# Two-layer hybrid trunk on one core: the second layer's gate projections first, their results kept in DRAM, and the triangular inverses moved wholly to VectorE beside them

## The chip, the cores and the metric

One core of a Trainium2 chip runs the whole program in one launch. The metric is the device time of that core in microseconds, as the median of three runs. TensorE (PE in the rows, PEld for its weight loads) multiplies matrices, VectorE (DVE) and ScalarE (ACT) do the elementwise work, GpSimd (POOL) does elementwise work and issues some DMAs, and SyncE's queue (SP) issues nearly all DMAs.

## What is computed

The trunk has two layers on a residual stream of 256 tokens by 2048 features, in float32. The second layer, which the change concerns, is:

```python
h = rms_norm(x, norm_g)
proj = einsum('btd,de->bte', h, w_in)                  # 2048 -> 18064 columns
q_c, ckv, z_c, iq, ik, iw, qkv, z_d, b_pre, a_pre = split_cols(proj, SPLIT_CD)
y_c = dsa_branch(q_c, ckv, z_c, ...)                   # sparse attention, 16 heads; ends  o * silu(z_c)
y_d = gdn_branch(qkv, z_d, b_pre, a_pre, ...)          # gated delta rule, 32 heads; ends  rms_norm(o) * silu(z_d)
x = x + einsum('bte,ed->btd', concatenate([y_c, y_d]), w_out)
```

The gates `silu(z_c)` (2048 columns) and `silu(z_d)` (4096 columns) are used only at the very end of each branch. The delta branch works in chunks of 64 tokens; in each chunk and head it solves a unit lower triangular 64 by 64 system:

```python
a_mat = where(strict, bc * kk * decay, 0.0)
sol = triangular_solve(eye + a_mat, concatenate([vb, kb]), lower=True, unit_diagonal=True)
```

With 32 heads and 4 chunks there are 128 such systems, one in each SBUF partition. The kernel forms the inverses and stores them.

## The kernel before

The kernel is one function that traces instructions for a planner: the planner gives each engine its own order, by the order in which instructions were traced and by its own estimate of when an operand is ready, and adds the waits. Matmuls that are traced inside `tick()` are pinned behind all matmuls traced before them; all others may be taken earlier when something ahead of them isn't ready.

Every projection multiplies float32 data as three fp32r products. `load_w` (line 179) loads 1 MB of weights into `wr` (3 buffers) on SP's queue, ScalarE casts them to `wh` and VectorE forms the rest `wl = wr - wh` (2 buffers each); both are traced at high priority. `proj_tok` (line 195) makes a 256-token by 512-column product with tokens in the partitions: for 2048 features 4 loads and 96 matmuls of 512 columns. `proj_feat` (line 227) makes its transpose: 4 loads and 192 matmuls of 256 columns. `out_proj` (line 343) takes 8 blocks of a finished unit through 4 times 512 columns of the output matrix, 192 matmuls of 512 columns in 8 loads, and adds to the residual.

Two kinds of background work are dealt into the projections. `steps` holds generators of which `tick()` (line 164) advances the first by one step; a projection calls `tick()` after each 4 (`proj_tok`: 2) blocks of matmuls, 16 times in a projection of 2048 features and 8 times for each 512 columns of `out_proj`. `flush()` runs all that is left. `lag(n)` is n empty steps. `bg` holds generators that `pump()` (line 151) advances by one step at each `load_w`; only the inverses are there.

The second layer's order is: keys, indexer, top-k and the latent `ckv`; then the inverses start (line 932); four attention groups; four delta groups of two halves; the last two output units and the final norm.

The inverses (lines 932 to 977) are 62 elimination steps on `U` (64 by 64 in each partition). Step s changes rows 0 to s-1 and columns s+1 to 63. POOL does the first 9 rows (`SPLIT = 9`), three instructions a step at lines 951, 952 and 954, all traced at once; VectorE does the other rows, two instructions a step at lines 962 and 964, one step at each `pump()` after four empty ones. At the end VectorE scales `U` (lines 968 and 970), POOL masks it (line 972), writes the diagonal (line 973) and stores it to `Wd` (line 974).

An attention group (line 990) projects queries `CQ` (192 matmuls), its keys and values from the latent (`w_uk`, `w_uv`, one load each), and its gate `CZC`; the generator `attend` (line 1017) runs four heads through logits, transposes and values, multiplies by the gate and turns the result into a unit. `qd`, `kd`, `vd` and `zc` have one buffer each, so a group waits for the group before to have ended its heads (line 992). Group 3 also does output unit 0.

A delta group i (line 1092) projects queries, and then for each half s: values (192 matmuls), `flush()`, the generator `delta` (line 1158), the gate `CZD` (96 matmuls, line 1246), and for s = 0 and i up to 2 the whole output unit i+1 (line 1251). `delta` is a chain: transposes `vt`, then for two 128-token parts the products `pu`, `pr`, `pu2`, `pog`, between them `pS`, `pks`, `pqs`, then a norm, the gate, and transposes `turn` (line 267).

Of the kernel before, what the change touches and what calls it, by code (L numbers as in the profile page):

```python
# [31 lines left out]
SPLIT = 9  # L32
# [3 lines left out]
LQ, LV, LS, LT = 7, 8, 2, 10  # L36
LH, LA = 3, 3
# [25 lines left out]
def trunk(ctx, tc, x, rel_bias, ab_norm, ab_w_in, ab_ml_b_i, ab_ml_b_f, ab_ml_norm, ab_ssm_conv_w,  # L63
# [107 lines left out]
    def lag(n):  # L171
        for _ in range(n):
            yield
# [550 lines left out]
    with ExitStack() as st:  # L724
# [189 lines left out]

        sv = ExitStack()
        sp = sv.enter_context(tc.tile_pool(name="sv", bufs=1))
        ap = sv.enter_context(tc.tile_pool(name="ap", bufs=1))

        cT = sp.tile([128, 4, 512], F32R, name="cT")
        cn = ap.tile([128, 2, 512], F32, name="cn", tag="zc")  # L920
        cs_ = ap.tile([128, 2], F32, name="cs_")
        cr = ap.tile([128, 2], F32, name="cr")
# [9 lines left out]
        U = sp.tile([128, 64, 64], F32, name="U")  # L932
        pl = sp.tile([128, 64], F32, name="pl")
# [8 lines left out]
        V.tensor_tensor(pl, pl, rl, op=OP.mult)  # L942
        V.tensor_tensor(wl_, pl, rl, op=OP.mult)  # L943
        V.tensor_scalar(nw, wl_, scalar1=-1.0, scalar2=None, op0=OP.mult)

        for s in range(1, 63):
            n, m = 63 - s, min(s, SPLIT)
            co = sp.tile([128, SPLIT], F32, name="co", tag="co")
            tmp = sp.tile([128, SPLIT * (63 - SPLIT)], F32, name="tmpg", tag="tmpg")
            tv = tmp[:, 0:m * n].rearrange("p (j l) -> p j l", j=m)  # L950
            G.tensor_scalar(co[:, 0:m], U[:, 0:m, s], scalar1=wl_[:, s:s + 1], scalar2=None, op0=OP.mult)  # L951
            G.tensor_tensor(tv, co[:, 0:m].unsqueeze(2).to_broadcast([128, m, n]),  # L952
                            U[:, s + 1:64, s].unsqueeze(1).to_broadcast([128, m, n]), op=OP.mult)
            G.tensor_tensor(U[:, 0:m, s + 1:64], U[:, 0:m, s + 1:64], tv, op=OP.subtract)  # L954

        def solve():
            yield from lag(LW)
            for s in range(SPLIT + 1, 63):
                n, m = 63 - s, s - SPLIT
                tmp = sp.tile([128, (63 - SPLIT) ** 2 // 4], F32, name="tmp", tag="tmp")  # L960
                tv = tmp[:, 0:m * n].rearrange("p (j l) -> p j l", j=m)
                V.scalar_tensor_tensor(tv, U[:, SPLIT:s, s:s + 1].to_broadcast([128, m, n]), wl_[:, s:s + 1],
                                       U[:, s + 1:64, s].unsqueeze(1).to_broadcast([128, m, n]), op0=OP.mult, op1=OP.mult)
                V.tensor_tensor(U[:, SPLIT:s, s + 1:64], U[:, SPLIT:s, s + 1:64], tv, op=OP.subtract)
                yield
            for i in range(4):
                Ui = U[:, i * 16:i * 16 + 16]
                V.tensor_tensor(Ui, Ui, nw.unsqueeze(1).to_broadcast([128, 16, 64]), op=OP.mult)
                yield
# [8 lines left out]

        Xc = [(cT, k) for k in range(4)]
# [6 lines left out]
        def out_unit(u, then=None):  # L986
            out_proj(cd_w_out, u * 1024, units[u], then)

        attended = []
        for g in range(4):  # L990
            pts = proj_feat(cd_w_in, 0, X, [(CQ + g * 512, 512, 0)])
            while len(attended) < g:
                tick()
            qd = ap.tile([128, 4, 256], F32, name="qd", tag="qd")
            for b in range(2):
                A.copy(qd[:, b * 2:b * 2 + 2].rearrange("p b t -> p (b t)"), pts[b])
            gated = []
            if g == 0:

                pts = proj_tok(cd_w_in, 0, X, CZC)  # L1000
                flush()
                zc = ap.tile([128, 2, 512], F32, name="zc", tag="zc")
                for t in range(2):
                    gate2(zc[:, t], pts[t])
                gated.append(True)
            pts = proj_feat(w_uk, 0, Xc, [(g * 512, 512, 0)])
            kd = ap.tile([128, 4, 256], F32, name="kd", tag="kd")
# [3 lines left out]
            vd = ap.tile([128, 2, 512], F32, name="vd", tag="vd")  # L1011
            A.copy(vd[:, 0], pts[0])
            A.copy(vd[:, 1], pts[1])
            if g:
                zc = ap.tile([128, 2, 512], F32, name="zc", tag="zc")

            def attend(g, qd, kd, vd, zc, gated):
# [51 lines left out]
                while not gated:  # L1069
                    yield  # L1070
# [7 lines left out]
            steps.append(attend(g, qd, kd, vd, zc, gated))  # L1078
            if g:
                pts = proj_tok(cd_w_in, 0, X, CZC + g * 512)  # L1080
                for t in range(2):
                    gate2(zc[:, t], pts[t])
                gated.append(True)
# [3 lines left out]
        if solving in bg:  # L1087
            drain(solving)
        sv.close()

        with tc.tile_pool(name="gp", bufs=1) as gp:
            for i in range(4):
# [23 lines left out]
                for s in range(2):  # L1116
# [39 lines left out]
                    gated = []  # L1156

                    def delta(s, h0, qc, kT, k0, QD, Wg, Kg, vf, o, z, rq, rq2, gated):
# [10 lines left out]
                        for t in range(2):  # L1169
                            A.activation(v[:, t], tp[t], AF.Copy, scale=0.5)  # L1170
                        yield from lag(LS)
# [62 lines left out]
                        while not gated:  # L1234
                            yield
# [87 lines left out]
```

## Time and profile before

| what | value |
|---|---|
| median of 3 runs | 2251.69 us (2250.92 to 2253.16) |
| the profiled execution | 2252.15 us |
| its span, first to last instruction | 2250.1 us |
| PE busy | 2148.8 us (95%) in 13006 matmuls |
| PEld busy | 1882.0 us (84%) |
| DVE busy | 1498.2 us (67%) |
| ACT busy | 999.1 us (44%) |
| POOL busy | 368.3 us (16%) |
| mean granted TensorE clock | 0.984 |
| HBM read, written | 382.51 MB, 19.03 MB |

The page gives busy times of each engine, the same in 40 equal slices of the span, the chain of waits that ended last, and groups of instructions. A matmul's busy time overlaps the next one's, so its price is the distance between two starts, not its mean. [...] The attention groups and the inverses lie between 1114 and 1425 us, the delta groups between 1425 and 2172 us.

### The profile page before, as it was taken

Reading aid. Unit: us, or ns where it says so; the run is one execution under the profiler, and the core shown is the slowest. Engines: PE = TensorE matmul, PEld = TensorE weight load, DVE = VectorE, ACT = ScalarE, POOL = GpSimd, SP = SyncE. Lnnn points to the kernel's source line nnn. Section 1 sums busy time; section 2 is a strip of 40 time slices with the busy share of each in tenths; the row PEclk is TensorE's granted clock in tenths of the full one; section 3 lists DMA queues with packets and bytes.
Section 4 is the critical chain, followed back from the end, with each engine's and each line's share of the span. In section 5 each row is a group of like instructions: output and inputs, shape, how many; then the busy total and the mean of one; then the engine's idle time right before and its main releaser. Section 6 shows DMA issues by size and latency. Waiting matters only on the chain.

```text
span 2250.1 us, 31828 instructions
## 1 busy us (share of the span) xinstructions
PE 2148.8 (95%) x13006; PEld 1882.0 (84%) x13006; DVE 1498.2 (67%) x2082; ACT 999.1 (44%) x1319; POOL 368.3 (16%) x352
## 2 busy tenths in 40 slices
PE   6999999999999998999967879999999999999997
PEld 6989997888788888988866768898997898888876
DVE  7898755545454557688699976565565657557655
ACT  5455444344434444556423335444454444345443
POOL 4000020000000003011399971000000000001001
PEclk9999999999999999999998989999999999999999
DMA  5655465555565554677833336665554554555443
GB/s 178 214 189 182 156 205 191 187 171 186 174 198 170 185 183 136 206 263 260 231 104 116 127 112 213 202 204 175 187 175 152 193 174 153 192 172 170 150 150 131
DMA packets 233992, 400.47 MB, mean 178 GB/s; under 512 B 39909, under 2 KB 63990, under 8 KB 232054
## 3 DMA queue, kind: packets, MB, share of 16 engines
q1 hardware_dynamic: 229046, 376.19, 51.0%
q0 software_dynamic: 4800, 22.25, 3.0%
q8 instruction: 102, 1.67, 0.3%
q14 instruction: 44, 0.36, 0.0%
HBM read 382.51 MB, written 19.03 MB: 178 GB/s over the span
## 4 chain that ended last, share of the span: by engine, by line
PE 77%; POOL 10%; DVE 4%; DMA 2%; ACT 2%; issue 1%; SPq 0%; ACTq 0%; DVEq 0%
PE pt L75 43%; PE pf L75 26%; POOL U L954 4%; POOL co L951 3%; POOL tmpg L952 3%; DVE wl L192 2%; PE pu L75 1%; ACT wh L191 1%; PE py L75 1%; DMA wr<-in_ab_w_in_dram 1%; DMA wr<-in_cd_w_in_dram 1%; PE turn L79 1%; PE pr L75 1%; PE pog L75 1%; PE si L75 1%
## 5 line engine op out<-in xcount | busy, mean ns | idle before, releaser
L192 DVE TENSOR_TENSOR wl<-wr,wh 128x2048 fp32r<-128x2048 f32 (+1 forms) x337 | 785.1, 2330 | 503.1 <-ACT wh L191 502.1
L191 ACT CAST wh<-wr 128x2048 fp32r<-128x2048 f32 (+1 forms) x337 | 639.3, 1897 | 769.7 <-PE pt L75 432.1
L75 PE MATMUL pf<-hT,wh 128*128 128x256 f32 x4192 | 771.5, 286 | 0.3 <-POOL hT L296 0.2
L75 PEld LDWEIGHTS pf<-hT,wh 128*128 128x128 f32 x4192 | 652.7, 191 | 12.0 <-issue 8.6
L75 PE MATMUL pf<-hT,wl 128*128 128x256 f32 x2096 | 593.2, 283 | 41.6 <-DVE wl L192 41.6
L75 PE MATMUL pt<-wh,hT 128*128 128x512 f32 x1856 | 605.4, 401 | 0.0
L75 PEld LDWEIGHTS pf<-hT,wl 128*128 128x128 f32 x2096 | 400.2, 191 | 44.9 <-DVE wl L192 44.1
L75 PEld LDWEIGHTS pt<-wh,hT 128*128 128x128 f32 x1856 | 349.6, 189 | 82.0 <-issue 2.1
L75 PE MATMUL pt<-wl,hT 128*128 128x512 f32 x928 | 370.0, 399 | 11.4 <-DVE wl L192 11.4
L75 PE MATMUL pt<-wh,uc 128*128 128x512 f32 x768 | 253.1, 399 | 0.0
L75 PEld LDWEIGHTS pt<-wl,hT 128*128 128x128 f32 x928 | 175.1, 189 | 55.6 <-DVE wl L192 14.8
L75 PEld LDWEIGHTS pt<-wh,uc 128*128 128x128 f32 x768 | 144.1, 188 | 33.4 <-issue 3.8
L75 PE MATMUL pt<-wl,uc 128*128 128x512 f32 x384 | 150.9, 393 | 0.0
L381 DVE SCALAR_TENSOR_TENSOR cy<-pf,gconv,cy 128x255 f32<-128x255 f32 (+2 forms) x192 | 88.2, 476 | 5.6 <-ACT cy L377 3.4
L1131 POOL TENSOR_TENSOR Kg<-Kg,rkb 64x512 f32<-64x512 f32 x8 | 10.3, 1284 | 497.4 <-DMA Kg<-KDd 260.6
L75 PEld LDWEIGHTS pt<-wl,uc 128*128 128x128 f32 x384 | 72.2, 188 | 14.5 <-issue 0.5
L75 PE MATMUL pt<-wh,ua 128*128 128x512 f32 x256 | 80.0, 392 | 0.0
L954 POOL TENSOR_TENSOR U<-U,tmpg 128x180 f32<-128x180 f32 (+59 forms) x62 | 78.7, 1269 | 4.9
L75 PE MATMUL pt<-wh,ub 128*128 128x512 f32 x256 | 79.1, 389 | 0.0
L350 DVE TENSOR_TENSOR xr<-pt,xr 128x512 f32<-128x512 f32 x80 | 55.0, 687 | 36.2 <-PE pt L75 36.1
L951 POOL TENSOR_SCALAR co<-U,wl__9050 128x9 f32<-128x9 f32 (+8 forms) x62 | 73.0, 1178 | 33.2 <-DVE wl__9050 L943 27.1
L296 POOL TENSOR_TENSOR hT<-xg,hT 128x512 fp32r<-128x512 f32 x24 | 41.4, 1737 | 201.2 <-issue 123.3
(445 smaller groups left out, 2111.2 us busy)
## 6 DMA issues: line engine op xcount, KB each, us to landing
wr<-in_cd_w_in_dram SPq DMA_DIRECT2D x140, 1024.0 KB, 5.0
wr<-in_ab_w_in_dram SPq DMA_DIRECT2D x87, 1024.0 KB, 5.1
wr<-in_cd_w_out_dram SPq DMA_DIRECT2D x48, 1024.0 KB, 5.0
wr<-in_ab_w_out_dram SPq DMA_DIRECT2D x32, 1024.0 KB, 5.1
wr<-in_ab_w_in_dram SPq DMA_DIRECT2D x33, 512.0 KB, 4.3
Dt<-gd SPq DMA_DIRECT2D x4, 1024.0 KB, 8.3
Dd<-Dt POOLq DMA_DIRECT2D x4, 1024.0 KB, 6.4
KDd<-KD POOLq DMA_DIRECT2D x4, 1024.0 KB, 11.3
```

The source lines that it names most:

```text
L75: return held(nc.tensor.matmul(*args, **kw))
L79: return held(nc.tensor.transpose(*args, **kw))
L191: A.copy(wh[:, 0:nk, 0:n], wr[:, 0:nk, 0:n])
L192: V.tensor_tensor(wl[:, 0:nk, 0:n], wr[:, 0:nk, 0:n], wh[:, 0:nk, 0:n].bitcast(F32), op=OP.subtract)
L296: L.tensor_tensor(hT[:, both, 256:512], part, hT[:, both, 0:256].bitcast(F32), op=OP.subtract)
L350: V.tensor_tensor(xc, pts[t], xc, op=OP.add)
L381: V.scalar_tensor_tensor(yi[:, s:256], u[:, 0:256 - s], tap(3 - s), yi[:, s:256], op0=OP.mult, op1=OP.add)
L951: G.tensor_scalar(co[:, 0:m], U[:, 0:m, s], scalar1=wl_[:, s:s + 1], scalar2=None, op0=OP.mult)
L952: G.tensor_tensor(tv, co[:, 0:m].unsqueeze(2).to_broadcast([128, m, n]), U[:, s + 1:64, s].unsqueeze(1).to_broadcast([128, m, n]), op=OP.mult)
L954: G.tensor_tensor(U[:, 0:m, s + 1:64], U[:, 0:m, s + 1:64], tv, op=OP.subtract)
L1131: G.tensor_tensor(Kg, Kg, rkb, op=OP.mult)
```

## The change

The gate projections of all twelve 512-column blocks (4 for attention, 8 for delta) come first, before any attention group. Each gate is made in a tile `zk` (2 buffers) and stored on SP's queue into a new DRAM tensor `zd`, one projection late. Attention and delta read it back with `gate_of` on SP's queue. The inverses run beside these projections, all 64 rows on VectorE: POOL's three instructions a step are gone, VectorE's two have all rows, and the one that makes the product is a plain multiplication of a column of `U` by a row of `Uw`, a copy of `U` scaled before. A step ends a `pump()` whenever 1150 elements have been done. The inverses' pool closes before the attention pool opens, whose `qd`, `kd`, `vd`, `zc` have two buffers. Output units 1 to 3 are dealt in two halves, two of four column blocks behind each half of a delta group. The numbers of empty steps are lowered.

```diff
-SPLIT = 9
-LQ, LV, LS, LT = 7, 8, 2, 10
-LH, LA = 3, 3
+STEPS = 1150
+LQ, LV, LS, LT = 5, 5, 2, 4
+LH, LA = 2, 3
-    def out_proj(w, r0, unit, then=None):
+    def out_proj(w, r0, unit, then=None, cols=range(4)):
-        for c in range(4):
+        for c in cols:
...
+        Uw = sp.tile([128, 64, 64], F32, name="Uw")
-        for s in range(1, 63):
-            n, m = 63 - s, min(s, SPLIT)
...
-            G.tensor_scalar(co[:, 0:m], U[:, 0:m, s], scalar1=wl_[:, s:s + 1], scalar2=None, op0=OP.mult)
-            G.tensor_tensor(tv, co[:, 0:m].unsqueeze(2).to_broadcast([128, m, n]),
-                            U[:, s + 1:64, s].unsqueeze(1).to_broadcast([128, m, n]), op=OP.mult)
-            G.tensor_tensor(U[:, 0:m, s + 1:64], U[:, 0:m, s + 1:64], tv, op=OP.subtract)
         def solve():
             yield from lag(LW)
-            for s in range(SPLIT + 1, 63):
...
-                V.scalar_tensor_tensor(tv, U[:, SPLIT:s, s:s + 1].to_broadcast([128, m, n]), wl_[:, s:s + 1],
-                                       U[:, s + 1:64, s].unsqueeze(1).to_broadcast([128, m, n]), op0=OP.mult, op1=OP.mult)
-                V.tensor_tensor(U[:, SPLIT:s, s + 1:64], U[:, SPLIT:s, s + 1:64], tv, op=OP.subtract)
-                yield
+            for i in range(4):
+                r = slice(i * 16, i * 16 + 16)
+                V.tensor_tensor(Uw[:, r], U[:, r], wl_[:, r].unsqueeze(2).to_broadcast([128, 16, 64]), op=OP.mult)
+                if i % 2:
+                    yield
+            done = 0
+            for s in range(1, 63):
+                n = 63 - s
+                row = Uw[:, s:s + 1, s + 1:64]
...
+                V.tensor_tensor(tv, U[:, 0:s, s:s + 1].to_broadcast([128, s, n]), row.to_broadcast([128, s, n]), op=OP.mult)
+                V.tensor_tensor(U[:, 0:s, s + 1:64], U[:, 0:s, s + 1:64], tv, op=OP.subtract)
+                done += s * n
+                if done >= STEPS:
+                    done -= STEPS
+                    yield
...
+        zd = dp.tile([12, 128, 1024], F32, name="zd")
+        for i in range(12):
+            pts = proj_tok(cd_w_in, 0, X, CZC + i * 512 if i < 4 else CZD + (i - 4) * 512)
+            keep()
+            z = sp.tile([128, 2, 512], F32, name="zk", tag="zk", bufs=2)
+            for t in range(2):
+                gate2(z[:, t], pts[t])
+            kept.append((i, z))
+        flush()
+        if solving in bg:
+            drain(solving)
+        keep()
+        sv.close()
...
-            while len(attended) < g:
+            while len(attended) < g - 1:
...
+            zc = ap.tile([128, 2, 512], F32, name="zc", tag="zc", bufs=2)
+            gate_of(g, zc)
...
-                    pts = proj_tok(cd_w_in, 0, X, CZD + h0 * 128)
-                    for c in range(2):
-                        gate2(z[:, c], pts[c])
-                    gated.append(True)
-                    if s == 0 and i <= 2:
-                        out_unit(i + 1)
+                    if i <= 2:
+                        out_unit(i + 1, cols=(0, 1) if s == 0 else (2, 3))
```

## Rows read from the trace of the kernel before

**Rows 1.** The page: busy tenths of engines and granted clock, 40 slices.

```profile
DVE  7898755545454557688699976565565657557655
POOL 4000020000000003011399971000000000001001
PEclk9999999999999999999998989999999999999999
```

**Rows 2.** Stretches: us, busy (instructions) of PE, PEld, DVE, ACT, POOL, clock, DMA share, GB/s.

```profile
1114.00:1331.00 217.00, 172.46 (x1013) 153.11 (x1012) 215.19 (x217) 78.70 (x121) 203.82 (x152) 0.91 0.38 124
1331.00:1351.00 20.00, 7.42 (x49) 7.22 (x48) 7.59 (x10) 2.39 (x4) 9.95 (x32) 0.66 0.16 50
...
1425.00:2170.00 745.00, 744.34 (x4671) 651.44 (x4670) 462.61 (x677) 340.24 (x498) 39.10 (x40) 1.00 0.53 174
```

**Rows 3.** Groups by form on PE, 1114 to 1351: count | busy, mean ns | idle before.

```profile
L75 PE MATMUL pf<-hT,wh 128*128 128x256 f32 x334 | 70.2, 310 | 0.0
L75 PE MATMUL pf<-hT,wl 128*128 128x256 f32 x166 | 51.9, 313 | 29.8 <-DVE wl L192 29.8
L75 PE MATMUL pt<-wh,hT 128*128 128x512 f32 x129 | 46.7, 426 | 0.0
L75 PE MATMUL pt<-wl,hT 128*128 128x512 f32 x64 | 26.9, 420 | 9.0 <-DVE wl L192 9.0
L75 PE MATMUL pf<-cT,wh 128*128 128x256 f32 x96 | 18.6, 293 | 0.0
L75 PE MATMUL pt<-wh,cT 128*128 128x512 f32 x48 | 16.9, 424 | 0.0
L75 PE MATMUL pf<-cT,wl 128*128 128x256 f32 x48 | 14.1, 294 | 2.2 <-DVE wl L192 2.2
L75 PE MATMUL pt<-wl,cT 128*128 128x512 f32 x24 | 10.6, 441 | 3.9 <-DVE wl L192 3.9
...
L79 PE MATMUL pp<-ident,L 128*128 128x128 f32 x33 | 7.6, 334 | 12.2 <-ACT L L1038 11.8 <-ACT L L1039 0.3
```

**Rows 4.** The chain of waits in order of time: start, length, instructions in it.

```profile
585.28 81.32 PE pt L75 x354
...
1448.37 33.61 PE pf L75 x288
```

**Rows 5.** Groups by line on DVE, 1114 to 1331, columns as in rows 3.

```profile
L962 DVE SCALAR_TENSOR_TENSOR tmp<-U,wl__9050 128x104 f32<-128x104 f32 (+26 forms) x52 | 73.2, 1407 | 1.1
L192 DVE TENSOR_TENSOR wl<-wr,wh 128x2048 fp32r<-128x2048 f32 x23 | 64.4, 2800 | 0.0
L964 DVE TENSOR_TENSOR U<-U,tmp 128x104 f32<-128x104 f32 (+26 forms) x52 | 47.8, 919 | 0.8
```

**Rows 6.** DVE in order of time at the inverses' end: start, length, idle before.

```profile
1343.66 1.23 DVE L968 TENSOR_TENSOR U<-U,nw 128x1024 f32<-128x1024 f32 x1 [12.41 <-POOL U L954]
...
1354.26 2.35 DVE L970 TENSOR_TENSOR U<-U,pl 128x1024 f32<-128x1024 f32 x2
```

**Rows 7.** DVE in order of time in a first-layer gate projection (`proj_tok`).

```profile
613.86 2.29 DVE L192 TENSOR_TENSOR wl<-wr,wh 128x2048 fp32r<-128x2048 f32 x1 [3.31 <-ACT wh L191]
...
621.67 0.68 DVE L388 SCALAR_TENSOR_TENSOR zg__5209<-zg__5209,pt 128x512 f32<-128x512 f32 x1
```

**Rows 8.** ACT in the same stretch as rows 7.

```profile
611.92 1.91 ACT L191 CAST wh<-wr 128x2048 fp32r<-128x2048 f32 x1 [3.69 <-PE pt L75]
```

**Rows 9.** PE in order of time in the last `delta`, projection matmuls left out.

```profile
2130.61 0.27 PE L79 MATMUL vt<-ident,vf 128*128 128x128 f32 x1
...
2159.20 1.05 PE L75 MATMUL pog<-u,QD 128*128 128x128 f32 x8
...
2167.99 0.30 PE L79 MATMUL turn<-ident,og__17926 128*128 128x128 f32 x1 [0.46 <-DVE og__17926 L1238]
```

**Rows 10.** POOL's mask of the inverses, line 972: duration min/median/max, start.

```profile
L972 POOL TENSOR_SCALAR_AFFINE_SELECT U<-U x1: 4071/4071/4071, 1361.2 to 1361.2; 128x4096 f32<-128x4096 f32 x1
```

**Rows 11.** DMA issues by line: count, size, us to landing.

```profile
Wd<-U POOLq DMA_DIRECT2D x1, 2048.0 KB, 11.2
```

More of the change, by code (lines that the diff above doesn't have):

```diff
@@ L977, in trunk, with keep, gate_of @@
         bg.append(solving)
+        zd = dp.tile([12, 128, 1024], F32, name="zd")
+        kept = []
+        def keep():
+            if kept:
+                i, z = kept.pop()
+                nc.sync.dma_start(zd[i].rearrange("p (t n) -> p t n", t=2), z)
+        for i in range(12):
[10 more added lines that the diff above has]
+        sv.close()
+        ap = at.enter_context(tc.tile_pool(name="ap", bufs=1))
+        def gate_of(i, dst):
+            nc.sync.dma_start(dst, zd[i].rearrange("p (t n) -> p t n", t=2))
         Xc = [(cT, k) for k in range(4)]
@@ L984, in new_unit, with out_unit @@
             units.append(yp.tile([128, 8, 512], F32R, name=f"uc{len(units)}", tag="u"))
-        def out_unit(u, then=None):
-            out_proj(cd_w_out, u * 1024, units[u], then)
+        def out_unit(u, then=None, cols=range(4)):
+            out_proj(cd_w_out, u * 1024, units[u], then, cols)
         attended = []
@@ L991, in trunk @@
             pts = proj_feat(cd_w_in, 0, X, [(CQ + g * 512, 512, 0)])
-            while len(attended) < g:
+            while len(attended) < g - 1:
                 tick()
-            qd = ap.tile([128, 4, 256], F32, name="qd", tag="qd")
+            qd = ap.tile([128, 4, 256], F32, name="qd", tag="qd", bufs=2)
             for b in range(2):
                 A.copy(qd[:, b * 2:b * 2 + 2].rearrange("p b t -> p (b t)"), pts[b])
[L997 to L1004, printed above, removed]
-                gated.append(True)
+            zc = ap.tile([128, 2, 512], F32, name="zc", tag="zc", bufs=2)
+            gate_of(g, zc)
             pts = proj_feat(w_uk, 0, Xc, [(g * 512, 512, 0)])
-            kd = ap.tile([128, 4, 256], F32, name="kd", tag="kd")
+            kd = ap.tile([128, 4, 256], F32, name="kd", tag="kd", bufs=2)
             for b in range(2):
@@ L1068, in attend @@
                 attended.append(g)
-                while not gated:
-                    yield
                 for t in range(2):
@@ L1076, in attend @@
                 yield from turning(y, units[-1], g % 2 * 4, 4, None)
[L1078 to L1083, printed above, removed]
+            steps.append(attend(g, qd, kd, vd, zc))
             if g == 3:
@@ L1086, in trunk @@
         flush()
[L1087 to L1089 removed]
+        at.close()
         with tc.tile_pool(name="gp", bufs=1) as gp:
@@ L1155, in trunk, with delta @@
                     z = gp.tile([128, 2, 512], F32, name="zg", tag="zg")
-                    gated = []
-                    def delta(s, h0, qc, kT, k0, QD, Wg, Kg, vf, o, z, rq, rq2, gated):
+                    def delta(s, h0, qc, kT, k0, QD, Wg, Kg, vf, o, z, rq, rq2):
                         hsl = [slice(h * 128, h * 128 + 128) for h in range(4)]
@@ L1170, in delta @@
                             A.activation(v[:, t], tp[t], AF.Copy, scale=0.5)
+                        gate_of(4 + h0 // 4, z)
                         yield from lag(LS)
@@ L1244, in trunk @@
                     flush()
-                    steps.append(delta(s, h0, qc, kT, k0, QD, Wg, Kg, vf, o, z, rq, rq2, gated))
-                    pts = proj_tok(cd_w_in, 0, X, CZD + h0 * 128)
-                    for c in range(2):
-                        gate2(z[:, c], pts[c])
-                    gated.append(True)
-                    if s == 0 and i <= 2:
-                        out_unit(i + 1)
+                    steps.append(delta(s, h0, qc, kT, k0, QD, Wg, Kg, vf, o, z, rq, rq2))
+                    if i <= 2:
+                        out_unit(i + 1, cols=(0, 1) if s == 0 else (2, 3))
             flush()
```

34 lines of the change are left out of this document (13 added, 21 removed).

## The prediction

> **What bounds the kernel now.** I read the 40 slices first [rows 1]: PE is busy nearly everywhere, and the one place where the granted clock leaves 1.00 for long is also the one where POOL is at 9 tenths and DVE at 9. Second the stretches [rows 2]. From 1425 to 2170 PE is busy 744.34 of 745 us at clock 1.00: the delta groups are bound by PE and have no stall to give back. From 1114 to 1351 (237 us: the inverses and the first attention groups) it is different: DVE 215 of 217 us, POOL 204 of 217, PE 172 of 217 and then 7 of 20, clock 0.91 and 0.66. Third, what PE did there [rows 3]: 500 projection matmuls of 256 columns and 193 of 512 on `hT`, 144 and 72 on `cT`. The chain of waits gives their prices in stretches without a wait, 33.61/288 = 0.117 us and 81.32/354 = 0.230 us [rows 4]: 58.4 + 44.3 + 16.8 + 16.5 = 136 us. The 153 other matmuls of the stretch (1013 + 49 of [rows 2], less 909) are small, 1.05/8 = 0.131 us [rows 9], 20 us. So 156 us of work took 237 us: **81 us are lost here**. [...]
>
> Why DVE is late: `wl` took 2.80 us there and 2.29 elsewhere [rows 5, 7]; line 964 took 47.8 us for some 26,180 elements, the sum of (s-9)(63-s), in 52 instructions [rows 5]: 1.49 ns an element after 0.17 us each, where a similar one without POOL beside it takes 1.23 us for 1024 [rows 6]. At the end DVE stood 12.4 us behind POOL's last step with a `wl` queued after it [rows 6].
>
> **The change, part by part.**
>
> *POOL's steps go.* All 186 POOL instructions and their hold on DVE's pace go, and with them the whole reason of the 81 us, if the new home of the inverses stays under PE's pace. Gain 81 us.
>
> *The gate stage.* Twelve projections of 4 groups of 24 matmuls. In a projection of the same form one group lasts 5.60 us (3.31 idle + 2.29 `wl`) [rows 7], so PE needs 48 x 5.60 = 269 us. DVE needs 48 x 2.29 = 110 for `wl`, 24 x 0.68 = 16 for the gates, and the inverses. From 1.23 us at 1024 and 2.29 at 2048 [rows 6, 7] an instruction costs 0.17 us + 1.035 ns an element. The sum of s(63-s) is 41,664; two passes in 124 instructions are 86.2 + 21.1 = 107 us; 4 instructions make `Uw` and 8 scale the end, 12 x 1.23 = 15; with the turned latent and small ones some 127 us. Together 253 of 269 us: it fits, at 94%. How closely: ACT's cast (1.91) and then `wl` (2.29) follow the release of a buffer and must end within 5.60 us [rows 7, 8], so `wl` may start 1.36 us late. 36 yields of 3.0 us (107/36) meet 3.0 us of free time (3.31 less 0.34 for gates). About a dozen yields hold two steps, up to 2 x 2.39 us; then 2.29 + 0.34 + 4.8 is 1.8 us over 5.60 and 0.5 over the allowance: 6 us, with a running backlog 8. Bounds 0 (single steps fall into the gaps; the planner also took steps early in the kernel before: 52 of the 53 were done by 1331 [rows 5], with group 3's loads still to come) and 20 (the stage dense from its start and each instruction 0.1 us dearer than the planner thinks). I take **+8**.
>
> *The end of the inverses.* POOL's mask takes 4.07 us [rows 10], then the diagonal, then 11.2 us to land `Wd` [rows 11]: some 18 us until `U`'s memory is free. The first thing written into the new pool is `qd`, one query projection (192 x 0.117 = 22 us) behind the last gate, and DVE ends a load or two before that. The read of `zc` waits for the same memory on SP's queue with the weights of `w_uk` behind it, and SP runs three loads (16 us) ahead; bounds 0 and 6, I take 0. Gate traffic is 12 x 0.5 MB out and in, each beside 22 us of matmuls; DMA share is 0.53 in a PE-bound stretch [rows 2]: 0.
>
> *Attention.* It loses the gate projection as cover: 24 ticks a group instead of 40, for a generator of 26 steps instead of 40; four groups need 104 to 108 ticks, three following groups and output unit 0 give 72 + 32. From logits to transposes 7 ticks of 12 x 0.117 = 1.4 us instead of 10. Queued on DVE and ACT ahead of a softmax stand at most a `wl` and a cast. Upper bound: the 12.2 us that PE lost to it while DVE was full [rows 3]; lower 0; I take **+4**.
>
> *Delta groups.* A half group loses 22 us of gate matmuls; output blocks are dealt to both halves. `delta` has 38 steps: half 0 meets 16 ticks of output and 16 of values, so its last steps fall into `flush()`; half 1 meets 16 + 16 + 16, less about 12 for norms and scores. The chain in its densest form took 37 us from `vt` to `turn` [rows 9], beside 57 us or more in each half (22 + 22 + some 13 of its own). SP: `gate_of` waits for `zg`'s only buffer with weight loads behind it, three loads ahead. What can be left bare is the wait for `turn` behind `flush()`, 7.7 us from the end of `pog` to `turn` [rows 9], four times: 31 us at most, 0 at least. In the row later output matmuls filled it to 0.46 us, so I take **+6**.
>
> *The tail.* In group 3 neither gates nor output units are left: half 0's remaining chain and half 1's whole one (about 28 + 37 us) meet their own 20 us and the 192 matmuls of unit 4, 44 us. Balanced; 0 to 8, I take **+3**.
>
> Everything else keeps its matmuls and their order. Sum: -81 + 8 + 4 + 6 + 3 = -60. Against the profiled execution, 2252.15 - 60 = 2192; the median of the runs shown is 0.46 us below that execution: 2191.7, **2192 us**.
>
> [...] Line 962 took 73.2 us for the same 26,180 elements as line 964: 2.46 ns an element [rows 5]. [...] No row shows 962's form without POOL, so I keep B.
>
> **Rivals.**
>
> A: nothing new is paid. 2252 - 81 = 2171. For it: delta groups without a stall [rows 2], dense chains that the planner fills to 0.46 us. Against it: DVE at 94% in the gate stage.
>
> B: the new product, with a column repeated along rows, isn't a 1.035 ns instruction. If POOL cost 962 what it cost 964 (1.49/1.035 = 1.44), its own price is 2.46/1.44 = 1.71 ns: DVE 253 + 28 = 281 us, 12 over PE. If 2.46 is its own: +59, 312 us, 43 over. Lost time came with clock, 81/57 = 1.42 a us of idle: 17 to 61 us in place of the 8. That gives 2201 to 2245. Against it: lines 968 and 970 repeat an operand too, and take 1.23 and 1.18 us for 1024 [rows 6].
>
> C (slower): the transposes `turn` aren't covered any more. Eight units and four attention groups end with 7.7 us from the last product to `turn` [rows 9], and the change has 4 ticks, 5.6 us, there instead of 10. If PE stands each time, 12 x 7.7 = 93 us: 2252 - 81 + 93 + 8 + 3 = 2275. It decides from about 9 of the 12 on (70 us, what is left of the gain). Against it: later matmuls may be taken ahead, as in the row.
>
> That the inverses aren't done within the 48 loads is a case of B: 4 + 2 + 36 + 4 yields need 46 or 47 of 48.
>
> **How the numbers follow.** Forecast 0.68 (own range 2180 to 2212, from its terms' bounds not all at one end), A 0.15, B 0.12, C 0.05, of which 0.02 beyond 9 of 12. The range 2172 to 2224 takes A's edge, the forecast and B's lower half, and leaves out B's upper half, C and what would lie below A. About 0.2% can be told from no change. Faster by more than that 0.97, within 0.01, slower 0.02.
>
> **What would show it.** Right: between about 1114 and 1385 POOL is empty, `wl` back to 2.29 us, the clock 1.00, PE's idle time behind `wl` under 10 us; the new product of 720 elements near 0.92 us; `pp` and `turn` waits of a few us in all; the delta stretch some 180 us (8 x 22.4) shorter, as its gates moved. Wrong: the product at 1.2 us or more for 720 elements (B); DVE 99% with the clock below 0.97 in the gate stage; idle time before `turn` of 5 us and more (C); idle time of PE before `w_uk`'s matmuls (the pool's release).

## The result, and the profile after

The changed kernel takes 2181.95 us (median of 4 runs, 2180.51 to 2185.32) against 2252.43 us (2250.92 to 2255.26) of the kernel before in the same stretch of time: a ratio of 0.9688, with a 95% interval of 0.9671 to 0.9705. The span of its profiled execution is 2178.8 us against 2250.1. The forecast was 2192, the sum was -60 us and the span fell by 71.3.

The page first, busy tenths and granted clock (in tenths of full speed) in 40 slices. They answer to [rows 1]: POOL's four slices of 7 to 9 tenths are gone, and the clock has no slice below 9 any more.

```profile
DVE  7888764545454557578879996556566666766765
POOL 4000020000000002201100001000000010100001
PEclk9999999999999999999999999999999999999999
```

The stretches of the second layer, in the columns of [rows 2]: the gate projections with the inverses, the 21 us behind them, the attention groups, the delta groups.

```profile
1085.00:1351.00 266.00, 265.53 (x1215) 217.12 (x1214) 237.15 (x212) 103.57 (x72) 8.87 (x3) 1.00 0.69 220
1351.00:1372.00 21.00, 16.64 (x107) 15.65 (x106) 7.69 (x5) 7.39 (x8) 0.00 (x0) 0.84 0.74 251
1372.00:1515.00 143.00, 143.00 (x1060) 135.69 (x1059) 81.67 (x124) 77.17 (x133) 0.00 (x0) 1.00 0.55 182
1515.00:2101.00 586.00, 583.20 (x3964) 520.28 (x3964) 386.68 (x630) 274.63 (x454) 40.98 (x40) 1.00 0.54 176
```

PE by line between 1114 and 1351 us, the stretch of [rows 3] (each group here has one form). There 57 us of idle time stood in the last column; here there is none.

```profile
L75 PE MATMUL pt<-wh,hT 128*128 128x512 f32 x627 | 197.2, 395 | 0.0
L75 PE MATMUL pt<-wl,hT 128*128 128x512 f32 x313 | 123.8, 395 | 0.0
L75 PE MATMUL pf<-hT,wh 128*128 128x256 f32 x103 | 18.1, 279 | 0.0
L75 PE MATMUL pf<-hT,wl 128*128 128x256 f32 x51 | 14.2, 279 | 0.0
```

DVE by line between 1100 and 1351 us, which answers to [rows 5]: `wl` is back from 2.80 to 2.30 us, and the 124 instructions of the elimination (all 64 rows now) take 106.2 us.

```profile
L192 DVE TENSOR_TENSOR wl<-wr,wh 128x2048 fp32r<-128x2048 f32 x45 | 103.6, 2303 | 19.2 <-ACT wh L191 18.5
L963 DVE TENSOR_TENSOR tmp<-U,Uw 128x62 f32<-128x62 f32 (+30 forms) x62 | 53.1, 856 | 1.1
L964 DVE TENSOR_TENSOR U<-U,tmp 128x62 f32<-128x62 f32 (+30 forms) x62 | 53.1, 856 | 1.2
```

One place still shows a loss: between 1351 and 1372 us PE is busy 16.64 of 21 us, at a granted clock of 0.84. To place such losses I took, for each kind of matmul, the median distance from its start to the next start in the kernel before, and added up by how much each distance in a trace differs from it, a shorter one counted as negative ("loss" below; this is my own sum over all 13006 matmuls, not a row). What remains of the span without it is 2109.1 to 2109.5 us in all fourteen traces of this study. That it stays the same is no finding, since the kernels have the same matmuls: the sum says where time is lost, and not why.

| loss, us | before | after |
|---|---|---|
| first layer | 21.3 | 19.8 |
| second layer up to the latent | 17.3 | 15.1 |
| gates, inverses, attention | 83.0 | 9.0 |
| delta groups and the rest | 19.1 | 25.8 |
| sum | 140.7 | 69.6 |

So the gain is where the prediction put it, 74 us, less 6.7 us in the delta groups. Another 3.7 us are ahead of the change, up to the latent; there the fourteen traces differ by 4 us among themselves, and this one is the lowest, so these 3.7 us are within that spread.

### The profile page after: what moved, and what is told of

Same layout as the page of the kernel before. It is cut to its first block, busy times and chain, and to the rows that moved or that the text cites. A ratio compares the mean times of both kernels' runs of the same rounds, so it can differ in the third digit from the quotient of the medians.

```text
span 2178.8 us, 31743 instructions
## 1 busy us (share of the span) xinstructions
PE 2133.9 (98%) x13006; PEld 1869.9 (86%) x13006; DVE 1467.0 (67%) x2104; ACT 997.5 (46%) x1319; POOL 156.7 (7%) x166
## 3 DMA queue, kind: packets, MB, share of 16 engines
HBM read 388.80 MB, written 25.32 MB: 190 GB/s over the span
## 4 chain that ended last, share of the span: by engine, by line
PE 88%; DVE 4%; DMA 2%; ACT 2%; issue 1%; POOL 0%; SPq 0%; ACTq 0%; DVEq 0%
PE pt L75 48%; PE pf L75 30%; DVE wl L192 2%; PE pu L75 2%; PE py L75 1%; ACT wh L191 1%; PE turn L79 1%; PE pr L75 1%; DMA wr<-in_cd_w_in_dram 1%; PE pog L75 1%; DMA zd<-zk 1%; PE si L75 1%; ACT Dt L860 1%; PE po L75 0%; PE lgt L75 0%
## 5 line engine op out<-in xcount | busy, mean ns | idle before, releaser
L192 DVE TENSOR_TENSOR wl<-wr,wh 128x2048 fp32r<-128x2048 f32 (+1 forms) x337 | 772.0, 2291 | 465.9 <-ACT wh L191 463.1
L75 PE MATMUL pf<-hT,wl 128*128 128x256 f32 x2096 | 589.9, 282 | 10.7 <-DVE wl L192 10.6
L75 PE MATMUL pt<-wh,hT 128*128 128x512 f32 x1856 | 593.0, 398 | 0.0
L381 DVE SCALAR_TENSOR_TENSOR cy<-pf,gconv,cy 128x255 f32<-128x255 f32 (+2 forms) x192 | 90.4, 476 | 12.8 <-ACT cy L377 11.2
L75 PEld LDWEIGHTS pt<-wh,ub 128*128 128x128 f32 x256 | 48.1, 188 | 10.1
L75 PEld LDWEIGHTS pt<-wh,ua 128*128 128x128 f32 x256 | 47.9, 188 | 9.6
L964 DVE TENSOR_TENSOR U<-U,tmp 128x62 f32<-128x62 f32 (+30 forms) x62 | 53.1, 856 | 1.2
```

The source lines that it names most:

```text
L75: return held(nc.tensor.matmul(*args, **kw))
L192: V.tensor_tensor(wl[:, 0:nk, 0:n], wr[:, 0:nk, 0:n], wh[:, 0:nk, 0:n].bitcast(F32), op=OP.subtract)
L381: V.scalar_tensor_tensor(yi[:, s:256], u[:, 0:256 - s], tap(3 - s), yi[:, s:256], op0=OP.mult, op1=OP.add)
L964: V.tensor_tensor(U[:, 0:s, s + 1:64], U[:, 0:s, s + 1:64], tv, op=OP.subtract)
```

## Experiments

Three things changed at once in the lost stretch: GpSimd's part went, the second operand of VectorE's product is read along a row instead of down a column, and the gate projections came first. The first experiments are corners of these three.

### The old order, all on VectorE: e5_old_order_all_dve

```diff
 # against the kernel before
-SPLIT = 9
+SPLIT = 0
-        for s in range(1, 63):
-            n, m = 63 - s, min(s, SPLIT)
...
-            G.tensor_tensor(U[:, 0:m, s + 1:64], U[:, 0:m, s + 1:64], tv, op=OP.subtract)
```

> The kernel before with all rows of the inverses on VectorE (SPLIT = 0, POOL's steps gone), everything else in the old order, the product still the three-operand instruction that reads a column. Theory (POOL): wl is back to 2.29 us; the solve is 107 us on DVE beside attention, where a load leaves some 2 us free, so DVE stays full and PE loses 10 to 30 of the 81 us: 2180 to 2205; the product takes about 1.04 ns an element. If the product's own price is 1.7 ns, 28 us more of DVE: 2205 to 2230. Rival (cover): without the gate projections in front the stretch loses 60 us or more: 2230 to 2255.

Measured: 2210.65 us, 42 below the kernel before (2252.95 in that stretch of time). DVE by line between 1100 and 1400 us (in this kernel the product is line 952, the subtraction 954):

```profile
L952 DVE SCALAR_TENSOR_TENSOR tmp<-U,wl__9050 128x62 f32<-128x62 f32 (+30 forms) x62 | 90.0, 1452 | 0.9
L954 DVE TENSOR_TENSOR U<-U,tmp 128x62 f32<-128x62 f32 (+30 forms) x62 | 53.2, 857 | 1.0
```

The subtraction is at the price that the prediction used. The old product is not, though GpSimd is silent: (90.0 - 62 x 0.17)/41,664 = 1.91 ns an element, against 2.46 beside GpSimd [rows 5] and 1.02 for the subtraction. So the product of the kernel before was dear by itself already, and taking GpSimd's part away brings 42 of the 71 us.

### The changed kernel with the column read: e10_column_read

```diff
 # against the changed kernel
-                V.tensor_tensor(Uw[:, r], U[:, r], wl_[:, r].unsqueeze(2).to_broadcast([128, 16, 64]), op=OP.mult)
+                V.tensor_tensor(Uw[:, r], U[:, r], wl_.unsqueeze(1).to_broadcast([128, 16, 64]), op=OP.mult)
-                row = Uw[:, s:s + 1, s + 1:64]
+                row = Uw[:, s + 1:64, s].unsqueeze(1)
```

> The changed kernel with one thing put back: the second operand of the elimination's product is again read down a column (64 elements of stride 256 bytes), still in a two-operand multiplication without a constant per partition and with nothing of it on GpSimd. Theory 1 (the stride sets the price): the 62 products take about 90 us instead of 53, VectorE has some 37 us more in the gate stage, where it has about 16 us to spare, and the time is 2195 to 2215. Theory 2 (the constant per partition, as third operand, sets the price): the products stay at 53 us and the time at 2182. If both have a part, the products fall between.

Measured: 2210.99 us, 29 above the changed kernel. DVE by line and shape, the product of 720 elements, first of the changed kernel, then of this one:

```profile
L963 DVE TENSOR_TENSOR tmp<-U,Uw 128x720 f32<-128x720 f32 x2 | 1.8, 902 | 0.0
```

```profile
L963 DVE TENSOR_TENSOR tmp<-U,Uw 128x720 f32<-128x720 f32 x2 | 3.0, 1484 | 0.0
```

Nothing differs between the two but the stride of one operand: 64 elements apart (256 bytes) the instruction takes 1.484 us, side by side 0.902. All 62 take 86.7 us instead of 53.1. The stretch from 1114 to 1351 us, and PE's waits from 1085 to 1515 us:

```profile
1114.00:1351.00 237.00, 218.44 (x902) 167.94 (x901) 234.34 (x186) 81.80 (x57) 0.00 (x0) 0.99 0.54 186
```

```profile
PE pt L75 <- DVE wl L192: 18.4, 22, 1.9
```

DVE is full (234 of 237 us) and PE waits behind `wl` 22 times: the prediction's rival B, which the change escapes only because it reads a row. B's working holds: 34 us more on DVE are 287 against PE's 269, and 18 x 1.42 (81 us lost for the 57 of idle time in [rows 3]) = 26 us; 29 were measured.

These runs read the operand 4 or 256 bytes apart and at no third stride, so how the price grows between the two, and why, they don't show.

### The old order with the row: e11_old_order_rows and e12_old_order_rows_timed

```diff
 # against e5_old_order_all_dve
-                                       U[:, s + 1:64, s].unsqueeze(1).to_broadcast([128, m, n]), op0=OP.mult, op1=OP.mult)
+                                       U[:, s:s + 1, s + 1:64].to_broadcast([128, m, n]), op0=OP.mult, op1=OP.mult)
```

> The kernel before with the inverses wholly on VectorE (as in e5_old_order_all_dve) and the product's column read replaced by the row that holds the same numbers, still with the constant per partition as third operand. Theory 1 (the stride sets the price): the 62 products take 53 us instead of 90, wl gets in sooner, and the loss of gates and attention falls from 36 us towards 15 to 25: 2187 to 2200 us. What is left above 2182 is then what the order of the gate projections brings. Theory 2 (third operand sets the price): 90 us and 2211 as e5. If the time is 2182, moving the gate projections and keeping their results brought nothing of its own.

Measured: 2175.1 us, 36 below e5 and below the changed kernel. The product by shape, and the stretch from 1114 to 1351 us:

```profile
L952 DVE SCALAR_TENSOR_TENSOR tmp<-U,wl__9050 128x720 f32<-128x720 f32 x2 | 1.9, 968 | 0.1
```

```profile
1114.00:1351.00 237.00, 235.93 (x1491) 211.50 (x1490) 233.09 (x297) 119.65 (x183) 0.00 (x0) 1.00 0.51 174
```

The constant per partition as a third operand costs 0.07 us in 720 elements (0.968 against 0.902), the stride 0.58. In the stretch PE is busy 235.93 of 237 us, with DVE at 98%: the old order keeps PE fed as well as the new one. I expected 2187 to 2200, with the rest as the order's gain; there is no such rest. So this kernel was timed beside the change:

> The kernel of e11_old_order_rows again, timed in rounds beside the changed kernel: the gate projections where they were before, the inverses wholly on VectorE, the product's row read. Theory (the order and the keeping of the gates bring nothing, they cost a few us): 2172 to 2178 us, 4 to 8 us under the changed kernel in the same stretch of time, with intervals against the kernel before that don't meet. Rival (the single look of 2175.1 was a fast one): 2180 to 2184, the same as the changed kernel.

> The changed kernel itself, timed beside e12_old_order_rows_timed: 2180 to 2184 us by every theory; it is there so that the two are compared on one chip.

Measured: 2176.45 us (2174.71 to 2181.32), ratio 0.9666 (0.9651 to 0.9681), beside 2182.96 us (2182.43 to 2187.08), ratio 0.9696 (0.9683 to 0.9709) of the changed kernel. The intervals just don't meet, and no run of the one lies among those of the other. Three edits in the kernel before beat the whole change by 6.5 us.

### The other corners: e14_rows_with_gpsimd and e4_new_order_split9

e14 is the kernel before with e11's one-operand edit alone, and GpSimd at work.

> The kernel before with nothing changed but the second operand of VectorE's product, which reads the row instead of the column; GpSimd keeps its nine rows of each step. It is the fourth corner beside the kernel before (GpSimd and column, 2252), e5 (no GpSimd, column, 2211) and e11 (no GpSimd, row, 2175). If the two savings are independent, VectorE's 52 products fall from 73 us to about 48 (as its subtractions, 1.5 ns an element beside GpSimd) and the time by 20 to 35 us, to 2215 to 2232. If GpSimd's last step, for which VectorE waited 12.4 us at the end, sets the end of the inverses, less comes back: 2235 to 2248. If the column read was slow only beside GpSimd, or the other way round, one of the two numbers is off by more than that.

Measured: 2231.41 us, 21 below before. DVE by shape, 720 elements, of e14 and then of the kernel before:

```profile
L964 DVE TENSOR_TENSOR U<-U,tmp 128x720 f32<-128x720 f32 x2 | 2.4, 1201 | 0.0
L962 DVE SCALAR_TENSOR_TENSOR tmp<-U,wl__9050 128x720 f32<-128x720 f32 x2 | 2.5, 1228 | 0.0
```

```profile
L962 DVE SCALAR_TENSOR_TENSOR tmp<-U,wl__9050 128x720 f32<-128x720 f32 x2 | 3.6, 1806 | 0.0
```

Beside GpSimd the row saves 0.58 us here too (1.806 to 1.228), and with GpSimd at work the product takes 0.26 more with a row or a column (0.968 to 1.228; 1.542 in e5 to 1.806) and the subtraction 0.30 (0.904 in e11 to 1.201), each as the mean of its two of 720 elements. Per instruction the two add up; in time they don't. At the end of the inverses VectorE still waits for GpSimd's last step, as long as before (12.41 us [rows 6]), only 21 us earlier:

```profile
1322.74 1.23 DVE L968 TENSOR_TENSOR U<-U,nw 128x1024 f32<-128x1024 f32 x1 [12.37 <-POOL U L954]
```

e4 is the changed kernel with the old inverses in it:

```diff
 # against the changed kernel
-STEPS = 1150
+SPLIT = 9
+            G.tensor_scalar(co[:, 0:m], U[:, 0:m, s], scalar1=wl_[:, s:s + 1], scalar2=None, op0=OP.mult)
+            G.tensor_tensor(tv, co[:, 0:m].unsqueeze(2).to_broadcast([128, m, n]),
...
-            for s in range(1, 63):
+            for s in range(SPLIT + 1, 63):
```

> The changed kernel's order (gate projections first, gates in DRAM, attention, delta) with the inverses of the kernel before: POOL does rows 0 to 8, VectorE the others with its old two instructions. Theory (POOL): the 81 us were lost because POOL's instructions slow DVE's two-input ones; beside the gate projections DVE has 48 wl at 2.8 = 134, 121 for its steps, 26 for gates and scaling, 281 us for PE's 269, and again a wait of some 12 us for POOL's last step, with clock: 30 to 60 us lost, 2210 to 2240; wl near 2.8 us. Rival (cover): what counted was to have the gate projections as cover and no softmax beside the inverses: then 2180 to 2190 and PE without idle time in the stage.

Measured: 2267.83 us, 15 above the kernel before, where I had expected a gain. The stretch, and DVE in order of time at the inverses' end:

```profile
1114.00:1351.00 237.00, 171.58 (x628) 130.52 (x627) 207.94 (x145) 56.05 (x38) 210.84 (x180) 0.86 0.41 131
```

```profile
1340.40 2.36 DVE L970 TENSOR_TENSOR U<-U,nw 128x1024 f32<-128x1024 f32 x2 [26.51 <-POOL U L956]
```

The old 12.41 us behind GpSimd [rows 6] have become 26.51, with a `wl` and so PE behind them (its longest wait is 26.8 us). All corners together, with the loss of gates, inverses and attention:

| GpSimd's rows | product reads | old order: us, loss | new order: us, loss |
|---|---|---|---|
| nine | column | 2252, 83.0 (before) | 2267.8, 94.2 (e4) |
| nine | row | 2231.4, 62.7 (e14) | not run |
| none | column | 2210.7, 36.4 (e5) | 2211.0, 35.1 (e10) |
| none | row | 2176.5, 3.5 (e12) | 2182.0, 9.0 (after) |

Down the columns: GpSimd's steps going is 42 to 57 us, the row 21 to 34 us. Across: the new order, with all that came with it (second buffers, steps dealt by elements, halved output units, fewer empty steps), is 15 us dearer, equal, and 6 us dearer; in no line does it gain. Every corner but e12, the change and the kernel before is a single run.

The losses in this table end with the attention groups, and that flatters the old order. In e5 and e12 the inverses' pool is closed only behind attention, and there SyncE's queue waits for the store of `U`, with weights queued behind. SP's waits in e12, 1350 to 1420 us:

```profile
SPq L1109 <- DMA Wd<-U: 11.4, 1, 11.4
```

PE loses some 5 us at that place, which the sum counts with the delta groups: 24.3 us in e5 and 23.8 in e12, against 19.1 in the kernel before. So the closed pool costs the old order some 5 us too, and most of the 6 us by which the change is dearer than e12 lies in its delta groups, 25.8 us.

### Is the elimination hidden? e3_no_elimination

```diff
 # against the changed kernel
-                V.tensor_tensor(tv, U[:, 0:s, s:s + 1].to_broadcast([128, s, n]), row.to_broadcast([128, s, n]), op=OP.mult)
-                V.tensor_tensor(U[:, 0:s, s + 1:64], U[:, 0:s, s + 1:64], tv, op=OP.subtract)
```

> The changed kernel without the 124 instructions of the 62 elimination steps (line 963 and 964): the triangular systems are not solved, all else stays. Theory (hidden): 106 us of DVE work beside the gate projections cost PE nothing, so nothing is won there; the store of U lands some 100 us earlier, so the stall at the end of the stage (4.5 us and about 3 us of clock) goes: about 2174. Rival (paid): the work costs PE time spread over the stage, 5 us or more: below 2170.

This kernel leaves the elimination out. Measured: 2178.8 us in a single run, 3 less for 106 us less of DVE. The elimination is hidden, and the gate stage has nothing left to give: from 1150 to 1351 us this kernel loses 1.1 us by the sum above, the changed one 1.0. What went is the stall at 1355 us, worth 6.7 us; 3.9 us are lost anew at 1141 us, where the mask now meets a `wl` (its rows stand in the last section), so gates and attention lose 5.9 instead of 9.0. DVE in order of time at 1355 us:

```profile
1351.61 2.29 DVE L192 TENSOR_TENSOR wl<-wr,wh 128x2048 fp32r<-128x2048 f32 x1 [3.31 <-ACT wh L191]
1357.51 0.56 DVE L1044 TENSOR_TENSOR bt<-bt,madd 128x384 f32<-128x384 f32 x1 [3.60 <-DMA bt<-bias_d]
```

### The stall at 1355 us: e1_zc_off_u and e9_bias_ahead

In the changed kernel the same two instructions stand the other way round. First POOL in order of time:

```profile
1329.91 6.05 POOL L974 TENSOR_SCALAR_AFFINE_SELECT U<-U 128x4096 f32<-128x4096 f32 x1 [246.91 <-DVE U L972]
1336.03 2.24 POOL L975 COPY U<-pl 128x64 f32<-128x64 f32 x1
1338.57 0.58 POOL L976 DMA_DIRECT2D Wd<-U  x1 [0.30 <-POOL U L975]
```

SP's queue in order of time, and its waits:

```profile
1352.82 0.34 SPq L1005 DMA_DIRECT2D zc<-zd  x1
1353.21 0.42 SPq L1044 DMA_DIRECT2D bt<-bias_d  x1
```

```profile
SPq L1005 <- DMA Wd<-U: 9.1, 1, 9.1
```

DVE in order of time:

```profile
1346.28 2.29 DVE L192 TENSOR_TENSOR wl<-wr,wh 128x2048 fp32r<-128x2048 f32 x1 [3.31 <-ACT wh L191]
1357.40 0.56 DVE L1046 TENSOR_TENSOR bt<-bt,madd 128x384 f32<-128x384 f32 x1 [8.83 <-DMA bt<-bias_d]
1357.88 2.28 DVE L192 TENSOR_TENSOR wl<-wr,wh 128x2048 fp32r<-128x2048 f32 x1
```

PE in order of time:

```profile
1355.46 0.40 PE L75 MATMUL pf<-cT,wh 128*128 128x256 f32 x2
1360.22 0.58 PE L75 MATMUL pf<-cT,wl 128*128 128x256 f32 x1 [4.36 <-DVE wl L192]
```

Read together: the mask and the diagonal end at 1338.3, the store of `U` is issued at 1338.57 and lands at 1352.5 (13.9 us); the read of the first gate waits for it on SP, the bias tile is queued behind the gate, the addition of the bias waits for its tile on DVE, and `wl` of `w_uk` is queued behind the addition. PE stands 4.4 us, and then runs at a granted clock of 0.50 to 1364.7, its 256-column matmuls 0.213 us apart instead of 0.117 (the granted clock is 0.50 for 6.8 us, from 1357.9 on). By the sum above this costs 6.7 us.

e1 makes the gate's tile lie on other memory than `U` had, to see whether the wait is for the address:

```diff
 # against the changed kernel: kd and vd are allocated ahead of zc
+            kd = ap.tile([128, 4, 256], F32, name="kd", tag="kd", bufs=2)
+            vd = ap.tile([128, 2, 512], F32, name="vd", tag="vd", bufs=2)
             zc = ap.tile([128, 2, 512], F32, name="zc", tag="zc", bufs=2)
```

> The changed kernel with the buffers of kd and vd set out ahead of those of zc in the attention pool, so that zc lies on Uw's old memory and not on U's; no instruction is added, removed or traced elsewhere. [...] Then the stall goes and the time falls by 6 to 8 us, to about 2175. Rival (order): the stall comes from the order on DVE, where the bias addition stands ahead of wl, and the bias load is late anyway: the stall stays, 2182.

Measured: 2182.19 us (2179.53 to 2184.47), ratio 0.9685 (0.9666 to 0.9703), the same as the change. SP's waits:

```profile
SPq L1005 <- DMA Wd<-U: 8.2, 1, 8.2
SPq L1005 <- DMA zd<-zk: 0.5, 1, 0.5
```

The read waits for `U`'s store still, on memory that by the order of allocation was not `U`'s (no trace shows the addresses). My theory of the address fell; as far as these runs go, the new pool's tiles wait until the whole closed pool is free. e9 takes both out of the closed pool's way:

```diff
 # against the changed kernel
-        cn = sp.tile([128, 2, 512], F32, name="cn")
+        cn = sp.tile([128, 2, 512], F32, name="cn", tag="zk", bufs=2)
-            gate_of(g, zc)
...
-                    bt = ap.tile([128, 384], F32, name="bt", tag="bt", bufs=2)
+                    bt = tp.tile([128, 384], F32, name="bt", tag="bt", bufs=2)
...
                 for k in range(6):
+                    if k == 2:
+                        gate_of(g, zc)
```

> The changed kernel with the attention's bias tiles in the pool that outlives the inverses (room for them comes from cn sharing the gates' two buffers), and with the reading of a group's gate traced two heads into the group instead of ahead of its projections, so that neither SyncE's queue nor VectorE's order meets the closed pool early. [...] Rival 1 (the next user of the closed pool, a copy of the queries on ScalarE or the first logits on VectorE, stalls instead): the stall moves some us later and the time stays at 2180 to 2183. Rival 2 (the stall was paid back later): no stall, same time.

Measured: 2182.77 us (2179.67 to 2187.39), ratio 0.9705 (0.9684 to 0.9726): no gain, where I had expected 2174 to 2177. The stall is gone:

```profile
1351.00:1372.00 21.00, 21.00 (x161) 20.08 (x160) 9.17 (x4) 9.62 (x9) 0.00 (x0) 1.00 0.90 348
```

But of the 6.7 us of the stall 5.6 are lost again ahead of it: from 1060 to 1110 us this kernel loses 8.9 us, the changed one 3.3. DVE in order of time, 270 us earlier:

```profile
1080.90 0.16 DVE L147 SCALAR_TENSOR_TENSOR cr<-nrq,cr 128x2 f32<-128x2 f32 x1
1081.91 0.56 DVE L1045 TENSOR_TENSOR bt<-bt,madd 128x384 f32<-128x384 f32 x1 [0.85 <-DMA bt<-bias_d]
1082.39 0.15 DVE L145 TENSOR_TENSOR nrq<-cr 128x2 f32<-128x2 f32 x1
...
1083.05 0.56 DVE L1045 TENSOR_TENSOR bt<-bt,madd 128x384 f32<-128x384 f32 x1
```

The planner, no longer held by the pool, put the first two bias additions into the middle of the latent's norm, a chain for which PE waits. From its first to its last instruction that chain takes 5.1 us here and 3.5 in the changed kernel, and PE's wait for the latent (`turn` behind `cn`) is 3.6 us in this trace and 1.3 in the change's (1.4 to 2.8 in the other traces of the new order); the rest is a lower granted clock behind that wait (0.59 from 1086 to 1090 us) and a wait of 1.8 us for a `wl` at 1104 us. Rival 1's time came, in another place: the stall was paid earlier, by an order that the edit set free.

### The delta groups: e7_old_lags and e8_out_whole

```diff
 # e7_old_lags, against the changed kernel
-LQ, LV, LS, LT = 5, 5, 2, 4
-LH, LA = 2, 3
+LQ, LV, LS, LT = 7, 8, 2, 10
+LH, LA = 3, 3
```

> The changed kernel with the spacing of the background steps in attention and delta units put back (queries 7, values 8, turn 10, heads 3 and attention 3, instead of 5, 5, 4, 2, 3). In the change the delta stretch lost about 6 us more than in the kernel before, spread over small gaps, where the prediction put +6 for units that begin while no gate projection stands between. Theory (the tighter spacing makes more changes between matmul forms and small gaps): the delta stretch's loss falls from 26.5 towards 20 to 23 us, and the time to 2176 to 2180, unless steps left over at the end are paid in the tail. Rival (the spacing fits the shorter stretch between units; with the old one the steps of a unit are drained bare ahead of the next): 2190 to 2215 us.

Measured: 2179.76 us in a single run. By the sum above the loss of the delta groups falls from 25.8 to 21.9 us (the expectations count 26.5 and 20.4 where the table has 25.8 and 19.1), that of gates and attention rises from 9.0 to 10.7. The first is as the theory said; the two together, 2 us, are too small for a single run.

```diff
 # e8_out_whole, against the changed kernel
-                    if i <= 2:
-                        out_unit(i + 1, cols=(0, 1) if s == 0 else (2, 3))
+                    if s == 0 and i <= 2:
+                        out_unit(i + 1)
```

> The changed kernel with each output projection of a finished unit put back in one piece (four column blocks behind the first delta unit of a pair, none behind the second). The delta stretch lost 26.5 us in the change against 20.4 in the kernel before. Theory (half a projection per unit is what covers a unit's chain of transposes and small matmuls now that no gate projection stands there): with none behind the second unit the stretch loses more, 30 to 50 us, and the time is 2185 to 2205. Rival (the background steps spread over the projections of the next unit anyway): the same within 3 us.

Measured: 2201.67 us, 20 above the change, the loss of the delta groups 42.9 instead of 25.8. PE's waits between 1515 and 2101 us:

```profile
PE pt L75 <- DVE wl L192: 6.8, 5, 1.8
PE pt L75 <- ACT wh L191: 4.0, 2, 2.0
```

In the changed kernel these waits are 0.4 us in all. Without the gate projections, the second half of a group needs its share of the output unit as cover; that part of the change pays for what the new order takes away.

## Why the prediction was right, point by point

**The gain of 81 us: right in size, its cause half right.** The loss of the stretch went from 83.0 to 9.0. The prediction gave the whole of it to GpSimd. The corners give GpSimd's steps 42 us and the row, on top, 34 (2210.65 to 2176.45). The step that failed is "the whole reason of the 81 us": it takes line 962's 2.46 ns an element [rows 5] for GpSimd's doing as well, and no row of the kernel before shows that form without GpSimd. It is 1.91 ns without (e5). The sum survived, by luck as far as the cause goes, since the change drops the column read together with GpSimd; had it kept it, rival B was the result, as e10 shows.

**The price of the new instructions: right.** 0.17 us + 1.035 ns an element gave 107 us for the 124 instructions, 106.2 were measured; 0.92 us for 720 elements, 0.902 measured.

**The gate stage, +8: too high.** From 1114 to 1351 us PE's idle time behind `wl` is 0.0. The whole stage up to 1351 us loses about 2 us by the sum, and e3 shows that the elimination has no part in it; so the term was near its lower bound, 0. The dozen yields with two steps, charged at 0.5 us each and more with a backlog, left no trace on PE. That the stage was nearly full is shown by e10: 34 us more on DVE were paid with 29.

**The end of the inverses, 0: wrong.** It cost 4.4 us of standing and, with the lower clock behind it, 6.7 of the 9.0, over the bound of 6. The step that failed is "the first thing written into the new pool is `qd`", with the thought that three loads ahead on SP are enough. The loads did run ahead (`w_uk`'s was issued at 1338.13). But the gate's read, issued at 1352.82, came before the copy of `qd` at 1352.90, the bias tile stood behind that read in the queue, and its addition ahead of `w_uk`'s `wl` on DVE; the prediction has no bias tile in it. The 18 us for the mask, the diagonal and the store were 22.6 (1329.91 to 1352.5): the mask took 6.05 us instead of 4.07 [rows 10] (the `wl` that it met stands in the last section), the store 13.9 instead of 11.2 [rows 11].

**Attention, +4: 0.** From 1372 to 1515 PE is busy 143.00 of 143 us, and the sum shows no loss from there to the last attention turn. The term was at its lower bound.

**Delta groups and tail, +9: 6.7.** The size was right, the place wasn't. The longest wait for `turn` in the delta groups is 0.5 us, so neither the 7.7 us of the term nor rival C's came; the loss is in many small gaps, and e7, a single run, puts 3.9 of it on the lower numbers of empty steps.

**The rest.** 3.7 us came from stretches that the change leaves alone (within their spread of 4 us between the traces here). From the last attention turn to the end of the span 807 us became 630, 177 less, where the prediction had 180 less 9. Term by term from -60: +7 at the pool, -6 at the gates, -4 at attention, -2 since 83 and not 81 were lost, -2 at delta and tail, -4 elsewhere: -71. The +7 hides as much of what the other terms had too high.

**What the prediction did not ask.** It took the new order for the cover that the inverses need. e11 and e12 show that they don't: with GpSimd silent and the row read, the old order keeps PE busy through the inverses as well (235.93 of 237 us in e11). With its own wait for the closed pool it loses some 8 us there, the new one 9.0.

## What to carry to other kernels

Where an instruction costs more per element than its neighbour of the same size, price its operands' strides before blaming the engine beside it; in a symmetric matrix the row holds what the column does, and one edited line was worth 21 to 34 us. When a change bundles several edits, run the corners: here two of them carried all of the gain, and the largest, the new order with what belongs to it, had none. Before a pool is closed ahead of other work, find on each engine the first instruction that touches the next pool and what is queued behind it; and when such a wait is lifted, look where the planner then puts the freed instruction.

## What the runs showed of the hardware

- A VectorE product in float32 whose one operand is read 256 bytes apart takes 1.48 us for 720 elements, with the elements side by side 0.90; over all 62 products 1.83 and 1.02 ns an element, each after 0.17 us. In the changed kernel an operand that repeats one element costs nothing more: the 62 products, which have one, and the 62 subtractions, which have none, take 53.1 us each.
- With GpSimd at work these 720-element instructions take 0.26 to 0.30 us more as the mean of two, the product by as much at either stride. One by one they differ: in the kernel before the two subtractions take 0.91 and 1.49 us, the two products 1.57 and 2.04.
- In the two traces shown here in which GpSimd's mask over `U` meets a `wl` of VectorE, the one that starts later takes longer by about the time in which they overlap. In the changed kernel `wl` starts first, and the mask, 4.07 us in the kernel before [rows 10], takes 6.05 (its row stands above, and ten of the fourteen traces have 6.05 or 6.06); in e3 the mask starts first, and `wl` takes 5.85 us instead of 2.29 and ends 2.13 us after the mask does. DVE in order of time, of the changed kernel and then of e3, and POOL of e3:

```profile
1329.75 2.28 DVE L192 TENSOR_TENSOR wl<-wr,wh 128x2048 fp32r<-128x2048 f32 x1
```

```profile
1135.07 5.85 DVE L192 TENSOR_TENSOR wl<-wr,wh 128x2048 fp32r<-128x2048 f32 x1 [0.43 <-ACT wh L191]
```

```profile
1134.72 4.07 POOL L972 TENSOR_SCALAR_AFFINE_SELECT U<-U 128x4096 f32<-128x4096 f32 x1 [49.96 <-DVE U L970]
```

  The overlap is 2.12 us in the changed kernel, where the mask is 1.98 longer, and 3.72 in e3, where `wl` is 3.56 longer.
- 12 x 0.5 MB of gates written and read again (HBM read 382.51 to 388.80 MB, written 19.03 to 25.32) cost PE no wait that the traces show, but for the one read behind the closed pool.
